# Expert gate and up products on one Trainium2 core: the token-lo blocks moved to the end of each bank, inside a branch of TensorE

## The chip, the cores and the metric

The kernel runs on one core of one Trainium2 chip. The metric is device time in microseconds (us) from the first to the last instruction; lower is better. All weights and inputs lie in DRAM as float32 when the kernel starts.

## The reference, cut to what matters

A two-layer decoder trunk over 256 tokens of width 1024. Layer 0 is a recurrent mixer with a dense SwiGLU, layer 1 a gated mixer with eight expert SwiGLUs of inner width 2816, of which every token uses the best two. The change concerns only the experts of layer 1:

```python
def swiglu(x, w_gu, w_down):
    gate, up = jnp.split(x @ w_gu, 2, axis=-1)
    return (jax.nn.silu(gate) * up) @ w_down

def moe_swiglu(x, w_router, w_gu, w_down):
    ...
    top_v, top_i = lax.top_k(logits, TOP_K)
    ...
    for e in range(N_EXPERTS):
        out = out + combine[:, e:e + 1] * swiglu(xt, w_gu[e], w_down[e]).astype(jnp.float32)
```

The 256 x 2 choices fall on all eight experts with the reference's own inputs (seed 0): 65, 55, 36, 28, 109, 103, 81 and 35 tokens, worked out from the reference's routing.

## The kernel before, in words

Every float32 product is made from rounded parts: a value is split into hi (rounded to the matmul's type) and lo (the rest), and a product is hi·hi + lo·hi + hi·lo, three matmuls into one accumulation in PSUM. For the experts the tokens of an expert are first gathered into 128 slots, which gives the blocks `xh` and `xl`, eight of each (128 rows of the 1024 each). These are the stationary side of the matmuls; the weights stream past them, 512 columns at a time.

The weights come by `Stream`. SP loads a piece of 2048 words a partition (1 MB) into one of the `raw` buffers. `part` (lines 119 to 128) splits 1024 words a partition of it: ScalarE writes the tile `hi` (line 127, `act.activation(h, v, AF.Copy)`), and then VectorE writes `lo` as the raw weights less `hi` (line 128). So a `lo` always follows its `hi`. The pool of `hi` tiles and the pool of `lo` tiles have four buffers each, by the 4 in line 831:

```python
    ws1 = Stream(ctx, "1", 1024, raws1, 4, "right")
```

An expert's `gate_up` (line 1162) goes over 2816 columns in five blocks of 512 and one of 256. For each it fills two PSUM banks called `gu`, first the gate, then the up columns. In this text a bank of 512 columns is a full bank, one of 256 a half bank. A full bank takes 1024 x 512 weights: four parts, each with two of the eight row blocks (k), and `lin_tm` (line 189) makes three matmuls for each row block, 24 in all. A half bank has two parts of four row blocks and also 24 matmuls, of 256 columns. `down` (line 1183) then takes 22 parts with six matmuls each, into the banks `py`.

`Feed.step` sets the order. It splits parts until those of this product are ready, issues the product, splits on until three parts (lead less one) of the next product are issued, calls `then()`, which issues what belongs to finished banks, and splits the fourth. `then()` after a gate bank issues the Silu on ScalarE (line 1176) and the transposes of the block before with their split (`hh` on ScalarE, line 224, `hl` on VectorE, line 225); after an up bank it issues the product of gate and up on VectorE (line 1178). In the first two steps of an expert it also issues the combination of the expert before (four matmuls and two VectorE additions a step, line 1256). ScalarE, VectorE and SP keep the order in which the program issues; TensorE's order is set by the scheduler.

After the experts a register is loaded from the largest count of tokens, and all engines jump over a second pass for experts with more than 128 tokens (lines 1298 to 1300).

Of the kernel before, what the change touches and what calls it, by code (L numbers as in the profile page):

```python
# [10 lines left out]
I32 = mybir.dt.int32  # L11
# [6 lines left out]
D = 1024  # L18
T = 256
KD = D // 128  # L20
# [12 lines left out]
def trunk(ctx: ExitStack, tc: tile.TileContext, a: dict, out: bass.AP, dbg=None, full=True):  # L33
# [31 lines left out]
    # ---------------------------------------------------------------- constants  # L65
# [12 lines left out]
    def preload(func):  # L78
        """The tables of an activation function, ahead of its first use."""
        act.activation(warm, ones[:, 0:1], func)  # L80
# [5 lines left out]
    # ---------------------------------------------------------------- weight stream  # L86
    class Stream:
        """Weights from DRAM in order, split into hi + lo parts of `size` words a partition."""
# [6 lines left out]
        def fetch(self, src):  # L95
            """Up to 2048 words a partition, [128, rows, columns]."""
            n1, n2 = src.shape[1], src.shape[2]
            raw = self.raws.pop(0)
            if raw not in self.once:
                self.raws.append(raw)  # L100
            v = raw()[:, :n1 * n2].rearrange("p (a b) -> p a b", a=n1)
            sp.dma_start(v, src)
            return v

        def split_parts(self, src, rows=None):
            """The parts of a piece of weights."""
            v = self.fetch(src)
            step = rows or self.size // v.shape[2]
            for k in range(0, v.shape[1], step):
                yield self.part(v[:, k:k + step, :])  # L110

        def fetch_cols(self, w, c0, n):
            """Columns c0..c0+n of w, in pieces of as many rows as fit."""
            if self.early:
                return self.early.pop(0)
            kk = min(KD, 2048 // n)
            return [self.fetch(w[k * 128:(k + kk) * 128, c0:c0 + n].rearrange("(k p) f -> p k f", p=128))
                    for k in range(0, KD, kk)]
# [12 lines left out]
        def blocks(self, w, c0, n):  # L131
            """Columns c0.. of w in blocks of 128, by rows k: [hi[k]], [lo[k]]."""
            vs = self.fetch_cols(w, c0, n)
            kk = vs[0].shape[1]
            width = min(n, max(128, self.size // kk))
            step = self.size // width
            for c in range(0, n, width):
                parts = [self.part(v[:, k:k + step, c:c + width]) for v in vs for k in range(0, kk, step)]
                for j in range(0, width, 128):
                    yield [[part[i][:, k, j:j + 128] for part in parts for k in range(step)] for i in range(2)]  # L140

        def cols(self, w, c0, n):
            """Columns c0..c0+n of w, by rows k: [hi[k]], [lo[k]]."""
            return self.split_cols(self.fetch_cols(w, c0, n))
# [6 lines left out]
        def rows(self, w, k0, nk):  # L151
            """Rows k0 * 128.. of w, by blocks of 128 rows."""
# [7 lines left out]
    class Feed:  # L160
        """Parts of weights, split `lead` parts ahead of their products."""
# [11 lines left out]
        def step(self, n, product, then):  # L173
            """The product with the next n parts; then() between the splits that come as these are used."""
# [7 lines left out]
    def lin_cm(o, w, x):  # L182
        """o[128 channels, T]: one block of 128 columns of w times x (hi and lo blocks)."""
        for k in range(KD):
            mm(o, w[0][k], x[0][k], k == 0, False)
            mm(o, w[1][k], x[0][k], False, False)
            mm(o, w[0][k], x[1][k], False, k == KD - 1)

    def lin_tm(o, w, x, t0, more=False):
        """o[128 tokens, columns]: x (hi and lo blocks) times columns of w."""  # L190
# [6 lines left out]
    def banks_cm(ws_, w, c0, n, x, piece=512, between=False):  # L197
        """Columns c0..c0+n of w times x, channels first: banks of two blocks; between: yields None between these."""
# [11 lines left out]
    def ahead(items):  # L210
        """The items, each once the one after it is under way."""
# [9 lines left out]
    def split(hi, lo, src, scale=None):  # L221
        """hi + lo = src * scale, exactly."""
# [7 lines left out]
    def rstd_of(pool_, ss, n, eps, name):  # L230
        """1 / sqrt(ss / n + eps)."""
# [10 lines left out]
    # ================================================================ layer 0: loads  # L242
# [43 lines left out]
    # ---------------------------------------------------------------- norms  # L286
    def rms(src, scr, both):
        """1 / rms of the rows of src [tokens, D]."""
# [9 lines left out]
    def turned(src, k, mm_bank):  # L298
        """Blocks k and k + 1 of src [tokens, D], channels first."""
# [6 lines left out]
    def normed(src, r, scaled, gain, n, mm_bank):  # L306
        """src * r * gain channels first, split; scaled: space for src * r."""
# [10 lines left out]
    class Norm:  # L318
        """RMS norm of xT as its blocks come: the blocks times the gain, split; the scale follows the products."""
# [7 lines left out]
        def squares(self, k, total):  # L327
            """total [128, 2, T]: the squares' sum over the blocks so far."""
# [10 lines left out]
        def scale(self, pl, ss=None):  # L339
            """1 / rms: a column per chunk of tokens, and across all partitions, twice."""  # L340
# [8 lines left out]
    # ---------------------------------------------------------------- memory attention  # L349
    def mem_kv(ws_, i, mh):  # L350
        """Yields between keys and values."""
# [9 lines left out]
    def mem_attn(i, qT, hi, lo, bank, sum_bank, tile, pr, together):  # L361
        """qT [128, 2, T] -> the two blocks hi, lo of the mixed activations; yields between pieces.
        tile(head), pr(head): space; together: all heads' scores before the first values."""
# [45 lines left out]
    # products that nothing reads, while x is loaded: they bring the tensor engine to its full clock  # L409
# [31 lines left out]
    # ================================================================ layer 0: time mixing  # L441
# [15 lines left out]
    def project(c0, whole):  # L457
        """Two blocks of columns; whole: in float32 as they are."""
# [64 lines left out]
    def per_head(o, r, n):  # L523
        """o[channels, n, 128 tokens] = r[tokens, 2 * n heads], each over its channels."""
# [66 lines left out]
    # inverses of the unit lower triangles: 16 rows by substitution, then merged in pairs, twice  # L591
    def fold(t):
        """24 pairs seen as two overlapping runs of 16: a leading dim of pairs to [2, 16]."""
# [32 lines left out]
    def block(out, l, r, i0, ni, c0, ncol, j0, nj):  # L626
        """out[i, c] = sum over j of l[i, j] * r[j, c], each given as (tile, offset, row's stride)."""
# [14 lines left out]
    # values, then values and keys tokens first, the values centered for the group norm  # L642
# [61 lines left out]
    # the states, chunk after chunk  # L704
# [35 lines left out]
    # the gate, times the group norm's weight, and times the bonus and the bias  # L740
# [27 lines left out]
    def group_norm(c0):  # L768
        """Group norm and gate of two chunks of tokens."""
# [21 lines left out]
    # memory keys and values of both layers, the attention of layer 0, and its mixed activations times w_out  # L791
# [18 lines left out]
    def mixed():  # L810
        """The mixed activations times w_out; yields between pieces of its columns."""
# [34 lines left out]
    # ---------------------------------------------------------------- dense SwiGLU  # L846
# [43 lines left out]
    # ================================================================ layer 1  # L890
# [87 lines left out]
    # ---------------------------------------------------------------- routing  # L978
# [11 lines left out]
    most_i = mr.tile([1, 1], I32, name="most_i")  # L990
    comb = mr.tile([128, 2, NE + 1], F32, name="comb")

    def slots(e0, base):
        """One-hot: the tokens of experts e0 and e0 + 1 in slots base.. ."""
# [11 lines left out]
    def routes(then):  # L1006
        """The two experts of each token, and its place among theirs."""
# [18 lines left out]
        dve.tensor_copy(most_i, most)  # L1026
        return dm, rest

    def gates():
        """The weights of the experts in the sum over them, and 1 / rms."""  # L1030
# [37 lines left out]
    def scaled(k, p):  # L1068
        """The block of columns times the gain; split, by what is returned."""
# [8 lines left out]
    def residual(k, p):  # L1078
        """Two blocks of the residual: with the mixed activations, in the routing's logits, and tokens first."""
# [36 lines left out]
    # ---------------------------------------------------------------- experts  # L1116
# [13 lines left out]
    def gather(e0, dm):  # L1130
        """The tokens of experts e0 and e0 + 1 in their slots: the experts' inputs, what makes a pair of blocks of
        these, and what makes the way back."""
# [29 lines left out]
    def gate_up(x, rs, hh, hl, step, at):  # L1162
        """silu(gate) * up, channels first, split. rs: 1 / rms of the slots' tokens."""
        for f in range(0, DFF, 512):
# [12 lines left out]
            step(KD * n // 1024, lambda w: lin_tm(ps[0], w, x, 0))  # L1177
            at(0, lambda: dve.scalar_tensor_tensor(sil, ps[1], rs, sil, op0=ALU.mult, op1=ALU.mult), True)
            at(1, turn)
            step(KD * n // 1024, lambda w: lin_tm(ps[1], w, x, 0))  # L1180

    def down(hh, hl, gw, step, at, last):
        """The expert's output, times the gates, split; last(o, c, y) for a half of its columns and a chunk of tokens."""
# [45 lines left out]
    def final_gain():  # L1229
        """In the space of a load."""  # L1230
# [7 lines left out]
    def finish(c, o):  # L1238
        """What the final norm can have before all squares are summed."""
# [18 lines left out]
    def experts(base, feed):  # L1258
        ahead_ = []

        def at(i, f, front=False):
            """f at the end of the step i from now."""
# [15 lines left out]
        for e in range(NE):  # L1278
# [5 lines left out]
            gate_up((xh, xl), gw[:, 1:2], hh, hl, step, at)  # L1284
# [17 lines left out]
    # ---------------------------------------------------------------- final norm  # L1302
# [34 lines left out]
```

## Time and profile before

| | |
|---|---|
| Median of 2 runs | 1339.28 us (1334.67 and 1343.89) |
| Profiled execution, its span | 1343.8 us (the run of 1343.89) |
| TensorE busy | 1312.2 us, 98% |
| VectorE busy | 1048.5 us, 78% |
| ScalarE busy | 894.8 us, 67% |
| DRAM to SBUF | 351 MB, 261 GB/s on average |
| The experts' stage | about 542 to 1330 us |

PE is TensorE's matmuls and PEld its loads of the stationary side, which overlap the matmuls; DVE is VectorE, ACT ScalarE. A matmul's end is modelled: matmuls are pipelined, and the time from start to start says what one takes in a row of them. [...]

### The profile page before, as it was taken

The page shows a single profiled execution, that of the slowest core. Times are in us where ns is not written, and L with a number is a line of the kernel's source. Part 1 is how long each engine was busy: PE and PEld are TensorE (multiplying, and loading weights), DVE is VectorE, ACT ScalarE, POOL GpSimd, SP SyncE. Part 2 cuts the span into 40 slices and gives each one's busy share as a digit, 9 for nine tenths or more (in the row PEclk, how much of TensorE's full clock was granted, in tenths as well). Part 3 has the DMA queues.
Part 4 walks back from the last instruction along what each step waited for, and adds up shares of the span by engine and source line. Part 5 has one row for each costly group of instructions (what it writes and reads, how often), then busy time and mean ns, then how long its engine had stood idle before and what let it go on. Part 6 is the DMA issues. An engine that isn't in the chain of part 4 may idle for free. (4 is left out here: it accounts for less than half of the span.)

```text
span 1343.8 us, 20395 instructions
## 1 busy us (share of the span) xinstructions
PE 1312.2 (98%) x7968; PEld 1130.8 (84%) x7968; DVE 1048.5 (78%) x1257; ACT 894.8 (67%) x1160; POOL 19.8 (1%) x40
## 2 busy tenths in 40 slices
PE   8998999999999998999999999999999999999996
PEld 7987778999999888788888888888888888888884
DVE  4789525666654775899997998997999987999996
ACT  6614416744443765887787887777777777777775
POOL 2000000000000100000000000000000000000000
PEclk8998959999999999999999999999999999999998
DMA  5512103755555844899999999999999999999970
GB/s 183 168 52 95 33 1 133 275 188 189 191 188 188 302 157 148 314 333 372 336 360 333 336 359 369 339 358 322 327 367 377 350 350 321 347 354 378 352 278 34
DMA packets 170648, 351.32 MB, mean 261 GB/s; under 512 B 5796, under 2 KB 46848, under 8 KB 170544
## 3 DMA queue, kind: packets, MB, share of 16 engines
q1 hardware_dynamic: 169216, 346.05, 72.7%
q0 software_dynamic: 1280, 3.88, 0.9%
q8 instruction: 64, 1.05, 0.3%
q14 instruction: 40, 0.33, 0.1%
q10 hardware_dynamic: 48, 0.01, 0.0%
HBM read 348.87 MB, written 1.05 MB: 260 GB/s over the span
## 5 line engine op out<-in xcount | busy, mean ns | idle before, releaser
L128 DVE TENSOR_TENSOR lo<-raw,hi 128x1024 fp32r<-128x1024 f32 (+1 forms) x636 | 737.0, 1201 | 140.0 <-ACT hi L127 138.6
L127 ACT ACTIVATE hi<-raw 128x1024 fp32r<-128x1024 f32 (+1 forms) x636 | 644.5, 1045 | 181.6 <-PE gu L58 58.4
L58 PE MATMUL gu<-hi,xh 128*128 128x512 f32 (+1 forms) x768 | 289.4, 377 | 0.0
L58 PE MATMUL gu<-hi,xl 128*128 128x512 f32 (+1 forms) x768 | 289.1, 376 | 0.0
L58 PE MATMUL gu<-lo,xh 128*128 128x512 f32 (+1 forms) x768 | 287.9, 377 | 0.0
L58 PEld LDWEIGHTS gu<-hi,xh 128*128 128x128 f32 x768 | 144.5, 188 | 27.9 <-ACT hi L127 0.2
L58 PEld LDWEIGHTS gu<-hi,xl 128*128 128x128 f32 x768 | 144.3, 188 | 28.0
L58 PEld LDWEIGHTS gu<-lo,xh 128*128 128x128 f32 x768 | 144.3, 188 | 27.4 <-DVE lo L128 0.2
L58 PE MATMUL lin<-nh,lo 128*128 128x256 f32 x528 | 151.6, 287 | 5.4 <-DVE lo L128 5.4
L58 PE MATMUL lin<-nh,hi 128*128 128x256 f32 x528 | 151.9, 288 | 0.5 <-DVE rT L446 0.2
L58 PE MATMUL lin<-nl,hi 128*128 128x256 f32 x528 | 151.0, 286 | 0.0
L58 PE MATMUL py<-hi,hh 128*128 128x512 f32 x352 | 140.4, 399 | 0.0
L58 PE MATMUL py<-hi,hl 128*128 128x512 f32 x352 | 139.5, 396 | 0.0
L58 PE MATMUL py<-lo,hh 128*128 128x512 f32 x352 | 111.1, 397 | 0.0
L58 PEld LDWEIGHTS lin<-nh,lo 128*128 128x128 f32 x528 | 101.3, 192 | 7.1 <-DVE lo L128 5.8
L58 PEld LDWEIGHTS lin<-nh,hi 128*128 128x128 f32 x528 | 101.2, 192 | 2.8 <-issue 0.7
L58 PEld LDWEIGHTS lin<-nl,hi 128*128 128x128 f32 x528 | 101.5, 192 | 1.0 <-issue 0.6
L58 PEld LDWEIGHTS py<-lo,hh 128*128 128x128 f32 x352 | 66.1, 188 | 16.3 <-DVE lo L128 0.5
L58 PEld LDWEIGHTS py<-hi,hh 128*128 128x128 f32 x352 | 66.3, 188 | 14.8
L58 PEld LDWEIGHTS py<-hi,hl 128*128 128x128 f32 x352 | 66.3, 188 | 14.8
L1176 ACT ACTIVATE sil<-gu,gw 128x512 f32<-128x512 f32 (+1 forms) x48 | 31.5, 655 | 42.7 <-PE gu L58 41.3
L225 DVE TENSOR_TENSOR hl<-mm,hh 128x512 fp32r<-128x512 f32 (+1 forms) x48 | 31.0, 646 | 25.8 <-ACT hh L224 25.8
(408 smaller groups left out, 1587.2 us busy)
## 6 DMA issues: line engine op xcount, KB each, us to landing
raw<-in_moe_w_gu SPq DMA_DIRECT2D x174, 1024.0 KB, 6.7
raw<-in_moe_w_down SPq DMA_DIRECT2D x87, 1024.0 KB, 6.9
raw<-in_ffn_w_gu SPq DMA_DIRECT2D x22, 1024.0 KB, 6.7
raw<-in_ffn_w_down SPq DMA_DIRECT2D x11, 1024.0 KB, 5.0
raw<-in_w_out SPq DMA_DIRECT2D x7, 1024.0 KB, 9.9
raw<-in_gmlp_w_in SPq DMA_DIRECT2D x7, 1024.0 KB, 5.3
raw<-in_rwkv_w_in SPq DMA_DIRECT2D x5, 1024.0 KB, 5.1
rawa<-in_rwkv_w_in SPq DMA_DIRECT2D x3, 1024.0 KB, 6.8
```

The costliest lines, as they stand in the source:

```text
L58: pe.matmul(o, l, r, start=start, stop=stop, skip_group_check=loose)
L127: act.activation(h, v, AF.Copy)
L128: dve.tensor_tensor(l, v, h.bitcast(F32), op=ALU.subtract)
L225: dve.tensor_tensor(lo, src, hi.bitcast(F32), op=ALU.subtract)
L1176: at(0, lambda: act.activation(sil, ps[0], AF.Silu, scale=rs), f > 0)
```

## The change

`gate_up` calls a new `lin_some` in place of `lin_tm`. For each of the eight row blocks it makes the two products of `xh` (with the weights' hi and with their lo); the eight products of `xl` with the weights' hi come after all of these, under a condition that the expert's count of tokens is above zero. The condition's body has TensorE's instructions alone. The counts, which the routing has in PSUM, are copied to integers on VectorE, and each expert loads its own into a register of TensorE. There are 96 such conditions in one pass over the experts, and eight register loads. The other engines get a plain jump at each of them. The diff also takes out comments and docstrings, which make no instruction.

```diff
@@ gate and up of an expert
-    def gate_up(x, rs, hh, hl, step, at):
+    def lin_some(o, w, x, n):
+        for k in range(KD):
+            mm(o, x[0][k], w[0][k], k == 0, False, True)
+            mm(o, x[0][k], w[1][k], False, k == KD - 1, True)
+        with tc.If(n > 0):
+            for k in range(KD):
+                mm(o, x[1][k], w[0][k], False, k == KD - 1, True)
+
+    def gate_up(x, rs, hh, hl, step, at, count):
...
-            step(KD * n // 1024, lambda w: lin_tm(ps[0], w, x, 0))
+            step(KD * n // 1024, lambda w: lin_some(ps[0], w, x, count))
...
-            step(KD * n // 1024, lambda w: lin_tm(ps[1], w, x, 0))
+            step(KD * n // 1024, lambda w: lin_some(ps[1], w, x, count))
@@ routing
+    count_i = mr.tile([1, NE], I32, name="count_i")
...
         dve.tensor_copy(most_i, most)
+        dve.tensor_copy(count_i, pl[0:1, 2 * NE:3 * NE])
@@ experts
-            gate_up((xh, xl), gw[:, 1:2], hh, hl, step, at)
+            count = nc.values_load(count_i[0:1, e:e + 1], engines=[mybir.EngineType.PE], min_val=0, max_val=T)
+            gate_up((xh, xl), gw[:, 1:2], hh, hl, step, at, count)
```

How the change moves instructions is seen at the second gate bank of the first expert. TensorE before, the last two of its four parts (`hi` and `lo` with neighbouring numbers are one part) and the start of the up bank behind it:

```order
L58 MATMUL gu_5727<-hi_5718,xh_5567 128x512
L58 MATMUL gu_5727<-hi_5718,xl_5568 128x512
L58 MATMUL gu_5727<-lo_5719,xh_5567 128x512
L58 MATMUL gu_5727<-hi_5723,xh_5567 128x512
L58 MATMUL gu_5727<-hi_5723,xl_5568 128x512
L1172 MATMUL mm_5771<-ident_83,sil_5624 128x128
L58 MATMUL gu_5727<-lo_5724,xh_5567 128x512
L58 MATMUL gu_5727<-hi_5723,xh_5567 128x512
L58 MATMUL gu_5727<-hi_5723,xl_5568 128x512
L58 MATMUL gu_5727<-lo_5724,xh_5567 128x512
```

Each part is used in six matmuls on end, and a part's `hi` is read for the last time at its fifth.

TensorE now, the same bank from its last part on, to the first matmuls of the up bank:

```order
L58 MATMUL gu_5741<-hi_5737,xh_5569 128x512
L1183 MATMUL mm_5786<-ident_83,sil_5636 128x128 x4
L58 MATMUL gu_5741<-lo_5738,xh_5569 128x512
L58 MATMUL gu_5741<-hi_5737,xh_5569 128x512
L58 MATMUL gu_5741<-lo_5738,xh_5569 128x512
L1169 COMPARE_AND_BRANCH
L58 MATMUL gu_5741<-hi_5722,xl_5570 128x512 x2
L58 MATMUL gu_5741<-hi_5726,xl_5570 128x512 x2
L58 MATMUL gu_5741<-hi_5732,xl_5570 128x512 x2
L58 MATMUL gu_5741<-hi_5737,xl_5570 128x512 x2
L1169 UNCONDITIONAL_BRANCH x2
L58 MATMUL gu_5742<-hi_5771,xh_5569 128x512
```

All four `hi` tiles of the bank are read once more behind the branch, the first of them (`hi_5722`) at the 17th and 18th matmul of 24. One of the two jumps ends the body, the other stands in the path of an expert without tokens.

ScalarE now, the four parts of this bank, and those of the up bank behind the jump:

```order
L127 ACTIVATE hi_5722<-raw11_5720 128x1024
L127 ACTIVATE hi_5726<-raw11_5720 128x1024
L127 ACTIVATE hi_5732<-raw20_5730 128x1024
L127 ACTIVATE hi_5737<-raw20_5730 128x1024
L1169 UNCONDITIONAL_BRANCH
L127 ACTIVATE hi_5771<-raw21_5769 128x1024
L127 ACTIVATE hi_5775<-raw21_5769 128x1024
L127 ACTIVATE hi_5781<-raw22_5779 128x1024
L1187 ACTIVATE sil_5743<-gu_5741,gw_5572 128x512
L224 ACTIVATE hh_5622<-mm_5786 128x512
L127 ACTIVATE hi_5793<-raw22_5779 128x1024
```

ScalarE's own order is as before but for the jump; with four buffers, `hi_5771` goes where `hi_5722` was.

## Rows read from the trace of the kernel before

**Rows 1.** Windows: stretch, busy us of PE, PEld, DVE, ACT, POOL, clock, DMA share, GB/s

```profile
600.00:700.00 100.00, 100.00 (x483) 82.72 (x482) 92.38 (x88) 78.67 (x84) 0.00 (x0) 1.00 0.99 359
```

**Rows 2.** Waits, 600 to 1300 us: who waited for whom, total us, times, longest

```profile
ACT hi L127 <- PE gu L58: 53.9, 130, 1.5
DVE lo L128 <- ACT hi L127: 47.8, 116, 3.2
...
PEld py L58 <- DVE lo L128: 0.5, 2, 0.3
```

**Rows 3.** Timeline of TensorE, two matmuls of one bank, start and length in us

```profile
645.75 0.40 PE L58 MATMUL gu<-hi,xl 128*128 128x512 f32 x1
...
648.77 0.39 PE L58 MATMUL gu<-lo,xh 128*128 128x512 f32 x1
```

**Rows 4.** Timeline of ScalarE in gate and up, with the idle time ahead

```profile
646.19 1.06 ACT L127 ACTIVATE hi<-raw 128x1024 fp32r<-128x1024 f32 x1 [0.33 <-PE gu L58]
...
655.70 0.69 ACT L1176 ACTIVATE sil<-gu,gw 128x512 f32<-128x512 f32 x1 [0.57 <-PE gu L58]
...
656.77 2.98 ACT L127 ACTIVATE hi<-raw 128x1024 fp32r<-128x1024 f32 x3
...
667.27 0.69 ACT L1176 ACTIVATE sil<-gu,gw 128x512 f32<-128x512 f32 x1 [0.57 <-PE gu L58]
```

**Rows 5.** Timeline of VectorE in gate and up

```profile
650.47 1.28 DVE L1256 TENSOR_TENSOR x<-mm,x 128x512 f32<-128x512 f32 x2
651.67 4.73 DVE L128 TENSOR_TENSOR lo<-raw,hi 128x1024 fp32r<-128x1024 f32 x4
...
657.86 4.63 DVE L128 TENSOR_TENSOR lo<-raw,hi 128x1024 fp32r<-128x1024 f32 x4 [0.26 <-ACT hi L127]
662.41 0.75 DVE L1178 SCALAR_TENSOR_TENSOR sil<-gu,gw,sil 128x512 f32<-128x512 f32 x1
663.07 3.51 DVE L128 TENSOR_TENSOR lo<-raw,hi 128x1024 fp32r<-128x1024 f32 x3
```

**Rows 6.** Timeline near the end: a split on the heels of ScalarE's copy

```profile
1317.18 1.07 ACT L127 ACTIVATE hi<-raw 128x1024 fp32r<-128x1024 f32 x1 [0.34 <-PE py L58]
...
1318.28 1.23 DVE L128 TENSOR_TENSOR lo<-raw,hi 128x1024 fp32r<-128x1024 f32 x1 [0.18 <-ACT hi L127]
```

**Rows 7.** Timeline near the end: TensorE starts again after a wait for VectorE

```profile
1330.19 0.74 DVE L228 SCALAR_TENSOR_TENSOR ys<-py,gw,ys 128x512 fp32r<-128x512 f32 x1
...
1330.99 0.72 PE L58 MATMUL gu<-ys,dT 128*128 128x512 f32 x2 [0.62 <-DVE ys L228]
```

**Rows 8.** Timeline of TensorE in a half bank

```profile
700.22 0.28 PE L58 MATMUL gu<-hi,xh 128*128 128x256 f32 x1
700.33 0.28 PE L58 MATMUL gu<-hi,xl 128*128 128x256 f32 x1
```

**Rows 9.** Timeline of VectorE across the register load and the jump behind the experts

```profile
1334.04 0.08 DVE L1246 DVE_READ_ACCUMULATOR sq<-x 128x1 f32 x1
1336.92 0.16 DVE L1304 TENSOR_TENSOR ss<-ssf 128x2 f32<-128x2 f32 x1 [2.81 <-DVEq L1299]
```

**Rows 10.** Timeline of TensorE's weight loads in the first gather

```profile
540.16 0.54 PEld L58 LDWEIGHTS gu<-dm,ngh 128*128 128x128 f32 x4 [0.42 <-ACT xh L1142]
```

**Rows 11.** Timeline of TensorE: two idle stretches in layer 0 and what ended them

```profile
28.13 1.31 PE L58 MATMUL mm<-lora,early 64*128 64x256 f32 x4 [1.57 <-ACT sg L504]
...
137.50 1.71 PE L58 MATMUL acc<-T,G 32*32 32x32 f32 x96 [1.25 <-DVE T L640]
```

**Rows 12.** Windows around these stretches, columns as in rows 1

```profile
28.40:28.80 0.40, 0.40 (x3) 0.34 (x3) 0.40 (x2) 0.40 (x3) 0.00 (x0) 1.00 0.00 0
...
29.20:29.60 0.40, 0.40 (x2) 0.23 (x2) 0.40 (x2) 0.40 (x2) 0.00 (x0) 0.50 0.00 0
...
32.40:32.80 0.40, 0.40 (x3) 0.35 (x3) 0.00 (x0) 0.40 (x1) 0.00 (x0) 1.00 0.00 0
...
138.50:139.00 0.50, 0.50 (x44) 0.50 (x38) 0.50 (x2) 0.45 (x2) 0.20 (x1) 1.00 0.00 0
```

## The prediction, made before the changed kernel was run

> **What bounds the kernel now.** I read the windows first. [...] Busy alone does not say who leads, so the waits come next: in 700 us of this stage ScalarE waits 53.9 us for TensorE to be done with a `hi` buffer, VectorE waits 47.8 us for ScalarE's `hi`, and TensorE's longest wait for a `lo` is one of 0.3 us, 0.5 us in all [rows 2]. So TensorE bounds the stage, and the split runs ahead of it, held back only by the four buffers. The timelines show the rhythm: a matmul of 512 columns every (648.77 - 645.75) / 13 = 0.232 us [rows 3]. A gate and an up bank together take 667.27 - 655.70 = 11.57 us from Silu to Silu, 5.79 us a bank [rows 4]; 48 matmuls are 11.14 of this, and the transposes the other 0.43.
>
> **The change part by part.** The number of matmuls is the same, and each row block is loaded as often as before. No expert of the reference's inputs is without tokens, so nothing is skipped. What changes is when a `hi` buffer comes free. Before, the first part of a bank is read for the last time at the 5th of 24 matmuls, the second at the 11th, and ScalarE can write the next bank's parts while this bank still runs. Now all four are read again at the end, the first until the 18th matmul, the fourth until the 24th. ScalarE cannot begin the next bank's first `hi` before the 18th, and VectorE's `lo` follows `hi`. TensorE needs that `lo` as the second matmul of the next bank. So the split no longer runs beside the bank before; most of it lies between the banks.
>
> The time from one bank's 18th matmul to the next bank's, step by step:
> - Release: the last matmul that reads a `hi` starts at 645.75, and ScalarE's next copy starts at 646.19: 0.44 us [rows 3, 4].
> - First `hi`: from its start at 1317.18 to the `lo` that waits for it at 1318.28, 1.10 us [rows 6].
> - VectorE's four `lo`: four on end take 4.63 us, and one alone 1.23, so a step is 1.13 [rows 5, 6]. Between the third and the fourth stands one other operation, the product of gate and up (from 662.41 to the next `lo` at 663.07, 0.66 [rows 5]) or the `hl` split, which I put at the same. From the first start to the fourth end: 3 x 1.13 + 0.66 + 1.23 = 5.28 us. ScalarE is faster: copies follow at (2.98 - 1.06) / 2 = 0.96 us, and with Silu and `hh` ahead of the fourth (655.70 to 656.77, 1.07) [rows 4] that one ends 5.0 us after the first starts, 0.1 us ahead of its `lo`.
> - TensorE starts again: 0.06 us after VectorE's end at 1330.93, and the pair there takes 0.72 us where 0.40 + 0.23 would do: 0.06 + 0.09 = 0.15 us [rows 7].
> - From the matmul with the fourth `lo` to the 18th: two more of the last row block, then two of `xl`, 4 x 0.232 = 0.93 us.
>
> Sum: 0.44 + 1.10 + 5.28 + 0.15 + 0.93 = 7.90 us, against 5.79, so +2.11 us. The transposes fit in TensorE's idle time: it gets to the fourth `lo` 0.4 us early with them in. An expert has nine such steps (ten full banks): 19.0 us.
>
> The half banks close the gate and up. From the last up bank's 18th matmul to their end, before: 6 x 0.232 + 48 x 0.116 [rows 8] + 0.43 = 7.4 us. Now the gate half's second `lo` is there after 0.44 + 1.10 + 1.13 + 1.23 = 3.90 us; with 0.15 to start, seven matmuls of the part, eight of `xl` and then the up half with the transposes (0.81, 0.93, 2.78, 0.43) the end is at 9.0: +1.6 us. In `down` nothing is moved: six matmuls a part are 1.39 us against VectorE's 1.13, and the split gets ahead again before the next expert.
>
> The combination of the expert before puts two additions (1.20 us, 650.47 to 651.67 [rows 5]) into VectorE's row in each of two steps, +1.7 us in all where the split is late; its eight matmuls, 1.86 us before, now fall into idle time. I count the two as equal.
>
> Together 8 x (19.0 + 1.6) = 165 us.
>
> The branches. Each bank has a compare ahead of `xl` and a jump behind. The order shows a wait of TensorE only in the path of an empty expert. When the compare comes, TensorE still has three matmuls of the last part, 0.70 us, and the jump has the eight of `xl`, 1.86 us; these hide both, and I take nothing. Without that cover, the nearest row bounds it from above: VectorE's 2.81 us behind the experts, which hold a register load, a compare and a jump over a whole second pass [rows 9]. The lower end is nothing. The jumps on ScalarE and VectorE come where both wait anyway.
>
> [...]
>
> The eight register loads stand in TensorE's queue in the first gather, around the products with `comb`. The lower end is nothing, since TensorE waits for ScalarE there anyway (0.42 us before 540.16 [rows 10]); the upper is 8 x 2.81 = 22 us [rows 9]. That row holds a load and more, so I take 1 us each, less what the wait hides: 7 us. SP has nothing new but jumps; loads are issued as `lo` frees the raw buffers, later than before, and the DMA engines get slack.
>
> Sum: 165 + 7 = 172 us on the profiled execution's 1343.9, 1516 us. That execution is 4.6 us above the median of the two runs shown, so on the median 1339.3 + 172 = 1511 us, 13% slower.
>
> **The rivals.**
>
> *The branches are not hidden.* A compare and a jump could hold TensorE's sequencer so long that the queue runs dry. For it: the 2.81 us on VectorE. Against it: that jump goes over a pass of hundreds of instructions, these over two. If each bank paid the whole row, less the 0.70 us of cover, 96 x 2.1 = 203 us come on top: about 1714; at half a microsecond beyond the cover, 1559.
>
> [...]
>
> *The clock falls.* Now TensorE idles about 0.9 us ahead of each bank's first `lo`, and some 2 us a bank in all. In layer 0 it idled 1.57 us until 28.13, and from 29.20 the clock was 0.50 (1.2 GHz), until it was full again at 32.40; an idle stretch of 1.25 us that ended at 137.50 left it at 1.00 [rows 11, 12]. Gaps of 0.9 us are shorter than both, which speaks against. If it fell in each bank for some 3 us, half of these, 1.6 us, would be lost, of which the idle time takes back up to 0.9: 0.7 to 1.6 us in 80 full banks, some 90 us: about 1600.
>
> *Not slower: the split still keeps ahead.* For it: TensorE hardly ever waits now, and ScalarE idles a fifth of the time. The step where it decides is the next bank's first `lo`: if this were ready when the 24th matmul has started and gone (6 x 0.232 = 1.4 us after the 18th), TensorE would go on as before. It would need a fifth buffer or an earlier release; the chain above has it at 0.44 + 1.10 + 1.23 = 2.8 us. Then only the loads remain: 1339 + 7 = 1346 us, within 2%.
>
> *The condition skips work.* With an empty expert eight of 24 matmuls go. But the four `lo` are still late: its step would lose only the two `xl` matmuls of 7.90, so even that expert would be slower than before. The counts have none; I give it nothing.
>
> **How the numbers follow.** The forecast has 0.72, the branches 0.10, the clock 0.12, not slower 0.03, and 0.03 is left for what I don't see (half of it faster by some rearrangement of TensorE's order). The forecast's own ends: a step shorter by 0.5 us (the restart hidden, the operation between the `lo` moved aside) is 36 us less, without the loads 43, so 1470 in round numbers; with 22 us of loads and 0.3 us more a step, 1550. The range goes on to 1610 to hold the clock's case and the smaller branch cases. A measurement can tell about 2% from no change (27 us): slower by more than that in all but the not-slower case and the remainder: slower 0.96, same 0.03, faster 0.01.
>
> **What would show it.** Right: TensorE's waits for `lo`, hardly there before, become the largest of the stage, about 2 us a full bank and over 100 us in all; ScalarE's copies come in runs of three and four right behind a bank's 18th matmul, where before one came every 1.4 us; Silu to Silu takes about 15.8 us; `down` takes as long as before; DMA share and VectorE's share fall. Wrong: idle time at the branch line with `lo` long ready (branches), a clock under 1.00 in the stage (clock), or Silu to Silu still near 11.6 us (not slower).

## The result, and the profile after the change

| | before | after |
|---|---|---|
| Median of 2 runs | 1339.28 us (1334.67 to 1343.89) | 1511.68 us (1509.03 to 1514.33) |
| Ratio, 95% interval | | 1.1246 (1.1170 to 1.1322) |
| Profiled execution, its span | 1343.8 us | 1512.5 us |

The changed kernel is slower by 12.5%; the forecast was 1511 us. First the same stretch of windows as in [rows 1], in the profile after:

```profile
600.00:700.00 100.00, 90.99 (x394) 66.95 (x392) 76.20 (x74) 62.84 (x69) 0.00 (x0) 1.00 0.87 302
```

TensorE makes 394 matmuls where it made 483, at the same granted clock of 1.00, the full one. In the whole execution it makes 7968, as before, so nothing was skipped. All the other engines and the DMA are less busy too, so none of them has become the bound: the stage has turned into a chain of waits. These are the waits of the same 700 us as in [rows 2]:

```profile
ACT hi L127 <- PE gu L58: 212.2, 69, 5.2
DVE lo L128 <- ACT hi L127: 181.9, 123, 2.6
PEld gu L58 <- DVE lo L128: 140.3, 215, 1.3
```

The first two were there before, at 53.9 and 47.8 us. The third is new: TensorE, which waited 0.5 us for `lo`, now waits 140 us with its weight loads. Fewer and longer waits of ScalarE (69 of up to 5.2 us, where it had 130 of up to 1.5) say that the `hi` buffers now come free in bunches.

One bank after the other shows it. In the timeline of the three engines the columns are start and length in us, engine, line and operation, and in brackets the idle time ahead and what ended it:

```profile
704.84 1.98 PE L58 MATMUL gu<-hi,xl 128*128 128x512 f32 x8
705.50 3.91 ACT L127 ACTIVATE hi<-raw 128x1024 fp32r<-128x1024 f32 x4 [2.86 <-PE gu L58]
706.59 3.50 DVE L128 TENSOR_TENSOR lo<-raw,hi 128x1024 fp32r<-128x1024 f32 x3 [2.60 <-ACT hi L127]
707.87 0.50 PE L58 MATMUL gu<-lo,xh 128*128 128x512 f32 x1 [0.77 <-DVE lo L128]
...
710.00 0.75 DVE L1189 SCALAR_TENSOR_TENSOR sil<-gu,gw,sil 128x512 f32<-128x512 f32 x1
...
710.66 1.22 DVE L128 TENSOR_TENSOR lo<-raw,hi 128x1024 fp32r<-128x1024 f32 x1
...
711.94 0.50 PE L58 MATMUL gu<-lo,xh 128*128 128x512 f32 x1 [0.16 <-DVE lo L128]
712.27 0.40 PE L58 MATMUL gu<-hi,xh 128*128 128x512 f32 x1
712.51 0.40 PE L58 MATMUL gu<-lo,xh 128*128 128x512 f32 x1
712.74 2.00 PE L58 MATMUL gu<-hi,xl 128*128 128x512 f32 x8
713.40 2.96 ACT L127 ACTIVATE hi<-raw 128x1024 fp32r<-128x1024 f32 x3 [4.00 <-PE gu L58]
```

The `xl` matmuls begin at 704.84. The second of them (704.84 + 0.23 = 705.07) is the last reader of the first `hi` tile, and only then, at 705.50, may ScalarE write the next bank's four parts, in one run. VectorE follows each, TensorE waits for every `lo` (the matmul behind such a wait shows 0.50 us: 707.87, 709.00, 710.14 and 711.94), and the eight `xl` follow the last pair without a gap: no idle time stands at the branch. Before, ScalarE's copies were spread over the bank and VectorE's four `lo` ran ahead of TensorE [rows 4, 5].

ScalarE's rows from the second expert's first bank on, and two Silu of gate banks:

```profile
664.40 2.96 ACT L127 ACTIVATE hi<-raw 128x1024 fp32r<-128x1024 f32 x3 [2.77 <-PE gu L58]
...
672.84 3.91 ACT L127 ACTIVATE hi<-raw 128x1024 fp32r<-128x1024 f32 x4 [3.96 <-PE gu L58]
...
681.94 2.96 ACT L127 ACTIVATE hi<-raw 128x1024 fp32r<-128x1024 f32 x3 [5.18 <-PE gu L58]
...
716.27 0.67 ACT L1187 ACTIVATE sil<-gu,gw 128x512 f32<-128x512 f32 x1
...
721.23 3.91 ACT L127 ACTIVATE hi<-raw 128x1024 fp32r<-128x1024 f32 x4 [2.86 <-PE gu L58]
...
732.00 0.67 ACT L1187 ACTIVATE sil<-gu,gw 128x512 f32<-128x512 f32 x1
```

Silu to Silu is 15.73 us, where [rows 4] had 11.57. The runs of copies follow each other after 7.90 us (705.50 to 713.40, with the product of gate and up in VectorE's row) and 7.83 us (713.40 to 721.23, with the `hl` split there): 7.87 us a bank on average, against 5.79.

### The profile page after: what moved, and what is told of

It reads as the page before. It is cut to its first block, busy times and chain, and to the rows that moved or that the text cites. A ratio compares the mean times of both kernels' runs of the same rounds, so it can differ in the third digit from the quotient of the medians.

```text
span 1512.5 us, 20557 instructions
## 1 busy us (share of the span) xinstructions
PE 1387.8 (92%) x7968; PEld 1111.4 (73%) x7968; DVE 1047.4 (69%) x1258; ACT 878.3 (58%) x1160; POOL 19.7 (1%) x40
## 5 line engine op out<-in xcount | busy, mean ns | idle before, releaser
L127 ACT ACTIVATE hi<-raw 128x1024 fp32r<-128x1024 f32 (+1 forms) x636 | 633.1, 1038 | 407.4 <-PE gu L58 287.8
L58 PE MATMUL gu<-lo,xh 128*128 128x512 f32 (+1 forms) x768 | 316.6, 418 | 91.0 <-DVE lo L128 91.0
L58 PE MATMUL gu<-hi,xl 128*128 128x512 f32 (+1 forms) x768 | 179.0, 376 | 0.0
L58 PEld LDWEIGHTS gu<-hi,xl 128*128 128x128 f32 x768 | 137.6, 189 | 27.4
L58 PE MATMUL acc<-hh,hi 128*128 128x256 f32 x132 | 36.8, 279 | 0.0
L58 PE MATMUL acc<-hh,lo 128*128 128x256 f32 x132 | 36.8, 279 | 0.0
```

The source lines that it names most:

```text
L58: pe.matmul(o, l, r, start=start, stop=stop, skip_group_check=loose)
```

## The experiments

Besides the median, each kernel is read by the time of one expert: the start of the first gate matmul of the second and of the eighth expert in its timeline of TensorE, a sixth of what lies between. This leaves out layer 0, after which the first expert starts anywhere from 531.58 to 553.88 us in these traces (last section), and the first expert itself.

| kernel | time, us | second expert | eighth expert | one expert, us |
|---|---|---|---|---|
| before | 1339.28 | 636.95 | 1232.11 | 99.19 |
| after | 1511.68 | 659.45 | 1380.22 | 120.13 |
| same order, no condition | 1513.35 | 657.52 | 1377.01 | 119.92 |
| conditions, old order | 1346.72 | 636.42 | 1231.42 | 99.17 |
| after, 5 `hi` buffers | 1440.98 | 659.13 | 1316.05 | 109.49 |
| after, 6 `hi` buffers | 1361.98 | 630.35 | 1244.24 | 102.31 |
| after, 8 `hi` buffers | 1361.77 | 637.34 | 1246.15 | 101.47 |
| after, operations behind the fourth split | 1452.18 | 652.64 | 1325.33 | 112.11 |
| after, both of the last two | 1347.66 | 640.43 | 1234.14 | 98.95 |

The rows of the kernel before and then of the changed one, on which the first two lines rest, with the first expert's start ahead of them:

```profile
542.20 0.40 PE L58 MATMUL gu<-hi,xh 128*128 128x512 f32 x1
...
636.95 0.40 PE L58 MATMUL gu<-hi,xh 128*128 128x512 f32 x1
...
1232.11 0.40 PE L58 MATMUL gu<-hi,xh 128*128 128x512 f32 x1
```

```profile
542.13 0.40 PE L58 MATMUL gu<-hi,xh 128*128 128x512 f32 x1
...
659.45 0.39 PE L58 MATMUL gu<-hi,xh 128*128 128x512 f32 x1
...
1380.22 0.39 PE L58 MATMUL gu<-hi,xh 128*128 128x512 f32 x1
```

The first four experiments below ran on one chip, beside 13 runs of the kernel before with a median of 1344.68 us (1333.73 to 1354.10); the last four on another, beside 13 with 1349.37 us (1340.31 to 1355.93).

**The order without the condition.** The `xl` matmuls stay last in the bank; the condition and the register loads go.

```diff
-        with tc.If(n > 0):
-            for k in range(KD):
-                mm(o, x[1][k], w[0][k], False, k == KD - 1, True)
+        for k in range(KD):
+            mm(o, x[1][k], w[0][k], False, k == KD - 1, True)
...
-            count = nc.values_load(count_i[0:1, e:e + 1], engines=[mybir.EngineType.PE], min_val=0, max_val=T)
+            count = None
```

Expected:

> The order of the changed kernel, with the xl products last in each bank, but without conditions, jumps and register loads. Buffer theory (the late release of the hi tiles costs the time): 1505 to 1517 us, Silu to Silu 15.7 us a pair of banks, as in the changed kernel. Branch rival (compares and jumps hold TensorE): back to 1339 to 1350 us, 11.6 us a pair.

Measured: 1513.35 us (one run), an expert 119.92 us. The largest wait of TensorE in 600 to 1300 us is that of the changed kernel:

```profile
PEld gu L58 <- DVE lo L128: 139.9, 214, 1.3
```

The order alone costs the loss. With the conditions an expert of twelve banks takes 0.21 us more, 0.02 us for each of them.

**The conditions without the order.** All 96 conditions and eight loads stay; only the last row block's `xl` matmul is inside, the other seven are back at their old places.

```diff
         for k in range(KD):
             mm(o, x[0][k], w[0][k], k == 0, False, True)
+            if k < KD - 1:
+                mm(o, x[1][k], w[0][k], False, False, True)
             mm(o, x[0][k], w[1][k], False, k == KD - 1, True)
         with tc.If(n > 0):
-            for k in range(KD):
-                mm(o, x[1][k], w[0][k], False, k == KD - 1, True)
+            mm(o, x[1][KD - 1], w[0][KD - 1], False, True, True)
```

Expected:

> 96 conditions and 8 register loads as in the changed kernel, but each holds only the xl product of the last row block; the other seven stand where they were. Buffer theory: hi tiles come free as before but for the fourth (24th matmul, not 23rd), so 1339 to 1350 us; what it is above the kernel before is the price of conditions, jumps and loads, which the prediction put at 7 us, all of it the loads. Branch rival: about 1512 us.

Measured: 1346.72 us (1342.42 to 1359.63, 10 runs), ratio to before 1.0036 (0.9994 to 1.0078). The first expert starts at 541.70 us (542.20 before), and TensorE is busy throughout; its windows, in the columns of [rows 1]:

```profile
600.00:700.00 100.00, 100.00 (x481) 82.66 (x480) 92.16 (x89) 78.65 (x85) 0.00 (x0) 1.00 0.98 359
```

This is the row of the kernel before but for a matmul or two, and an expert takes 99.17 us against 99.19. Twelve conditions an expert cost nothing that can be seen here, where matmuls stand queued on both sides of them.

**Eight `hi` buffers.** If the late release is the cause, a second set of four buffers takes it away. Two of the ten raw buffers go for the room.

```diff
-    ws1 = Stream(ctx, "1", 1024, raws1, 4, "right")
+    ws1 = Stream(ctx, "1", 1024, raws1, 4, "right", 8)
...
-    ws.raws += [raw_buffer(ctx, f"raw2{i}", 2048, "right") for i in range(4)]
+    ws.raws += [raw_buffer(ctx, f"raw2{i}", 2048, "right") for i in range(2)]
```

(The new last argument sets the buffers of `hi` alone.) Expected:

> The changed kernel with eight hi buffers in place of four (the space comes from two of ten raw buffers). Buffer theory: the next bank's hi tiles have places of their own, the split runs beside the bank before, 1340 to 1360 us. Branch rival: stays at 1505 to 1520 us.

Measured: 1361.77 us (one run), 2 us above the range given: 150 of the 172 us are back, by the expert 18.7 of 20.9, with the order and the conditions as in the changed kernel. What is left shows in the waits (600 to 1300 us) and in ScalarE's timeline:

```profile
ACT sil L1187 <- PE gu L58: 118.7, 41, 4.4
...
PEld gu L58 <- ACT hi L127: 16.8, 27, 0.8
```

```profile
773.20 0.69 ACT L1187 ACTIVATE sil<-gu,gw 128x512 f32<-128x512 f32 x1 [3.26 <-PE gu L58]
...
774.26 7.72 ACT L127 ACTIVATE hi<-raw 128x1024 fp32r<-128x1024 f32 x8
785.25 0.69 ACT L1187 ACTIVATE sil<-gu,gw 128x512 f32<-128x512 f32 x1 [3.27 <-PE gu L58]
```

ScalarE, now ahead, stands at the Silu for 3.3 us until the gate bank is finished, and the fourth `hi` of the next bank stands behind it in the program's order. Silu to Silu is 12.05 us, 0.48 over [rows 4]; five such pairs in each of eight experts are 19 us. TensorE's waits for `hi` come about once a pair (27 in 700 us, in which seven experts make 35 pairs). The last experiment tries this reading.

**The kernel before with two raw buffers fewer**, the control for the room:

```diff
-    ws.raws += [raw_buffer(ctx, f"raw2{i}", 2048, "right") for i in range(4)]
+    ws.raws += [raw_buffer(ctx, f"raw2{i}", 2048, "right") for i in range(2)]
```

Expected:

> Control: the kernel before with the same two raw buffers taken away and nothing else. Both theories: 1335 to 1355 us, since TensorE bounds the experts and the loads have eight raw buffers left.

Measured: 1341.58 us (one run), inside the range of the kernel before; an expert takes 99.21 us (632.37 to 1227.61 for six). The room that the buffers took is not what the other runs show.

**Five `hi` buffers**, the edit above with 5 in place of 8. Expected:

> The changed kernel with five hi buffers in place of four (and two of the ten raw buffers fewer, which room this takes and which by itself cost nothing). Theory (the late release of the hi buffers sets the step): the next bank's first hi needs no release any more, its second waits for the release at the 18th matmul, so only three lo and the one other operation follow the release: 0.44 + 1.10 + (2 x 1.13 + 0.66 + 1.23 = 4.15) + 0.15 + 0.93 = 6.77 us a bank in place of 7.90, 1.13 less; over 72 steps 81 us less than the changed kernel: about 1425 us (1400 to 1440). Silu to Silu 13.5 us. ScalarE's wait for TensorE falls from 267 us to about 190. Rival (what costs is the order of the matmuls in itself, or the lo being needed as the second matmul, whatever the buffers): 1500 to 1515 us.

Measured: 1440.98 us (one run), 1 us above the range given. The step itself is as worked out: ScalarE's copies behind a release start at these times,

```profile
692.92 2.01 ACT L127 ACTIVATE hi<-raw 128x1024 fp32r<-128x1024 f32 x2 [2.85 <-PE gu L58]
...
706.50 2.01 ACT L127 ACTIVATE hi<-raw 128x1024 fp32r<-128x1024 f32 x2 [2.88 <-PE gu L58]
```

13.58 us for two banks (one more run starts between them, at 699.72), 6.79 a bank against 6.77 expected. The experts only started later, at 553.88 us where before had 542.20; without these 11.7 us it would be 1429. They come from layer 0, whose granted clock was lower in this execution (last section).

**Six `hi` buffers.** Expected:

> The changed kernel with six hi buffers (two raw buffers fewer). Theory: two lo and the other operation follow the release, 0.44 + 1.10 + (1.13 + 0.66 + 1.23 = 3.02) + 0.15 + 0.93 = 5.64 us, under the 5.79 us that the 24 matmuls and transposes take, so TensorE is the bound again: 1340 to 1375 us, as with eight buffers (1361.8). Silu to Silu 11.6 to 12.0 us. Rival (each further buffer brings the same until eight): about 1425 less another 30 to 40, 1390 us.

Measured: 1361.98 us (one run), an expert 102.31 us. That this is the time of eight buffers is chance: the experts began at 531.58 us here and at 538.51 there, and 0.84 us more for each expert take up this lead. The gain does not come buffer by buffer: four to five brings 10.6 us an expert, five to six 7.2, six to eight 0.8. It ends about where the chain, by the sum above 5.64 us, gets shorter than the 5.79 us of a bank's matmuls and transposes.

**The operations of finished banks behind the fourth split**, with four `hi` buffers:

```diff
-            self.upto(self.lead - 1)
-            then()
             self.upto(self.lead)
+            then()
```

Expected:

> The changed kernel with four hi buffers, but the operations that belong to finished banks (Silu and hh on ScalarE, the product of gate and up and hl on VectorE) issued after the fourth split of the next bank and not between the third and the fourth. Theory (VectorE's row of four lo with the one operation in it lies wholly between the banks): 0.66 us less a step, 7.24 us, so 72 x 0.66 = 48 us less than the changed kernel: about 1464 us (1450 to 1480), Silu to Silu 14.5 us. Rival (the step hangs on ScalarE's copies, or on TensorE's release alone): 1500 to 1515 us.

Measured: 1452.18 us (one run), 12 us less than worked out. ScalarE's runs start at

```profile
693.24 3.90 ACT L127 ACTIVATE hi<-raw 128x1024 fp32r<-128x1024 f32 x4 [2.30 <-PE gu L58]
700.47 3.90 ACT L127 ACTIVATE hi<-raw 128x1024 fp32r<-128x1024 f32 x4 [3.32 <-PE gu L58]
```

7.23 us apart, against 7.24 expected: one VectorE operation of 0.66 us in the row of `lo` was worth exactly its time. An expert takes 8.0 us less; nine steps of 0.66 are 5.9. I had left out that the combination's additions go behind the fourth split too. In the changed kernel they lengthen the second expert's first two steps by 1.80 us (next section); here these two are as short as the others, 7.23 and 7.25 us:

```profile
657.03 3.91 ACT L127 ACTIVATE hi<-raw 128x1024 fp32r<-128x1024 f32 x4 [2.44 <-PE gu L58]
...
664.26 3.90 ACT L127 ACTIVATE hi<-raw 128x1024 fp32r<-128x1024 f32 x4 [2.76 <-PE gu L58]
671.51 3.90 ACT L127 ACTIVATE hi<-raw 128x1024 fp32r<-128x1024 f32 x4 [3.34 <-PE gu L58]
```

5.9 and 1.80 are 7.7 of the 8.0 us.

**Eight `hi` buffers and the operations behind the fourth split**, both edits. Expected:

> The changed kernel with eight hi buffers and with the operations of finished banks issued after the fourth split. With eight buffers alone 1361.8 us were left, 17 to 20 more than before. Theory for that rest (ScalarE keeps its order, waits for a bank's end at the Silu, and only then writes the fourth hi of the next bank, for which TensorE then waits): the fourth hi is written ahead of the Silu, TensorE does not wait, and the time is that of the kernel before, 1335 to 1350 us, with TensorE's waits for hi (25 us with eight buffers alone) near nothing. Rival (the conditions, or something else that the order brings, costs the rest): 1358 to 1365 us.

Measured: 1347.66 us (1336.61 to 1359.14, 10 runs), ratio to before 0.9961 (0.9912 to 1.0009). Its Silu and copies:

```profile
760.66 0.69 ACT L1186 ACTIVATE sil<-gu,gw 128x512 f32<-128x512 f32 x1 [3.48 <-PE gu L58]
...
772.20 0.69 ACT L1186 ACTIVATE sil<-gu,gw 128x512 f32<-128x512 f32 x1 [2.56 <-PE gu L58]
```

ScalarE still stands at the Silu, but now nothing that TensorE needs next is behind it: Silu to Silu is 11.54 us again and an expert 98.95. From 600 to 1300 us TensorE's gate and up no longer wait for a `hi`. In the first expert they still do (7.1 us in all), and that one takes 98.78 us where it took 94.75 before. So with the new order, all conditions and all loads in place, the kernel is as fast as before once the buffers and the order of ScalarE let the split run ahead. It is no faster: TensorE has the same matmuls to make and is the bound again, and no kernel tried here beat the one before.

## Why the prediction was right, step by step

**What bounds the kernel.** Confirmed. TensorE led before [rows 1, 2], and what it lost is what the kernel lost.

**The step of a full bank.** The five terms, forecast and read from the timeline above:

| term | forecast | measured | from |
|---|---|---|---|
| release | 0.44 | 0.43 | 705.07 to 705.50 |
| first `hi` | 1.10 | 1.09 | 705.50 to 706.59 |
| four `lo` and the one operation | 5.28 | 5.29 | 706.59 to 710.66 + 1.22 = 711.88 |
| TensorE starts again | 0.15 | 0.16 | 711.88 to 711.94, and 0.33 where 0.23 would do |
| last four matmuls | 0.93 | 0.93 | 711.94 to 712.74 + 0.23, less 0.10 |
| sum | 7.90 | 7.90 | with the `hl` split in place of the product 7.83 |

Each term came from a row of the kernel before in which the same hand-over happened once by itself, and each held to within 0.01 us.

**The half banks.** Two rows each, of the kernel before and of the changed one, bound this part: the matmul that is the last full bank's 18th (or, after, the first of the `xl` row, of which the 18th is the second), and the first of `down`:

```profile
694.62 0.40 PE L58 MATMUL gu<-lo,xh 128*128 128x512 f32 x1
...
702.33 0.39 PE L58 MATMUL py<-hi,hh 128*128 128x512 f32 x1
```

```profile
736.31 1.98 PE L58 MATMUL gu<-hi,xl 128*128 128x512 f32 x8
...
746.01 0.39 PE L58 MATMUL py<-hi,hh 128*128 128x512 f32 x1
```

After: 746.01 - 736.54 = 9.47 us, of which two `py` matmuls that the scheduler put in between take 0.46, so 9.0 as forecast. Before: 7.71 us, not 7.4; I had left out the 18th matmul's own 0.23 us. The difference is 1.3, not 1.6. `down` takes as long as before, as forecast: from its first matmul to the third expert's first 738.51 - 702.33 = 36.2 us before, 781.94 - 746.01 = 35.9 after, with those two matmuls of 0.46 us already made.

**The combination.** Forecast: 1.7 us in VectorE's row, given back by its matmuls falling into idle time. The two steps that hold it run from 664.40 to 672.84 and to 681.94: 8.44 and 9.10, together 1.80 us over two plain ones.

**The branches.** Forecast nothing, and next to nothing was found, three times over: taken away (119.92 us an expert against 120.13), put in alone (99.17 against 99.19), and with the order repaired (98.95). The bound of 2.81 us from the jump behind the experts [rows 9] was far too high for these short jumps. The trace of the changed kernel has them on the queue of TensorE's weight loads (PEldq). The columns are the count, then the shortest, middle and longest in ns, then the first and last start in us; the second line has 711 to 713 us alone, the bank shown in the result:

```profile
L1169 PEldq COMPARE_BRANCH  x192: 65/130/307, 542.5 to 1464.5; - x192
...
L1169 PEldq COMPARE_BRANCH  x2: 65/117/169, 711.9 to 712.1; - x2
```

Each condition has two jumps. Both of this bank have ended by 712.3 us, while the matmuls ahead of `xl` still run; the first `xl` starts at 712.74. The cover that I named, matmuls queued on both sides, is there in all three kernels; a condition without it was not tried.

The two of this bank take 0.065 and 0.169 us, 0.23 together. Twelve such pairs would be 2.8 us an expert (an estimate from these two times), if TensorE had to stand still for them; the 99.17 us against 99.19 say that it did not.

**The register loads.** This is the term that was mis-sized: 7 us forecast, 1.0 us found at most. The trace of the changed kernel has all eight, 0.30 us each and the first 0.49, and the kernel before had one on the same queue, behind the experts, a nearer row than [rows 9]:

```profile
L1295 PEldq TENSOR_LOAD <-count_i x8: 297/304/491, 534.2 to 539.4; - x8
```

```profile
L1298 PEldq TENSOR_LOAD <-most_i x1: 487/487/487, 1331.1 to 1331.1; - x1
```

They run beside the matmuls of the first gather. From the gather's first matmul to the first gate matmul TensorE takes 542.13 - 534.00 = 8.13 us with them, and 541.22 - 534.08 = 7.14 us in the kernel without conditions and loads. Part of this 1.0 us is the clock, which in the second kernel was back at 1.00 some half a microsecond earlier (0.76 against 0.52 from 537 to 538 us). That the wait for ScalarE in the gather [rows 10] covers the rest of the loads is the likely reason; no run took that wait away. The first expert's start by itself (542.13 us with loads, 542.20 before) does not tell, since it has all of layer 0 in it.

**What I missed.** The first expert takes 659.45 - 542.13 = 117.32 us against 636.95 - 542.20 = 94.75: 22.6 more, where the others take 20.9 more. From one bank's `xl` to the next, its first two steps last 9.17 and 8.96 us (545.87 to 555.04, and to 564.00), without any combination:

```profile
545.87 1.99 PE L58 MATMUL gu<-hi,xl 128*128 128x512 f32 x8
...
551.29 0.69 ACT L1187 ACTIVATE sil<-gu,gw 128x512 f32<-128x512 f32 x1 [1.32 <-DVE gw L1155]
551.87 1.05 ACT L127 ACTIVATE hi<-raw 128x1024 fp32r<-128x1024 f32 x1
552.97 0.51 PE L58 MATMUL gu<-hi,xh 128*128 128x512 f32 x1 [0.84 <-ACT hi L127]
...
555.04 3.57 PE L58 MATMUL gu<-hi,xl 128*128 128x512 f32 x8
...
558.45 0.40 PE L58 MATMUL gu<-hi,xh 128*128 128x512 f32 x1
```

```profile
555.00:558.00 3.00, 3.00 (x8) 2.33 (x7) 0.73 (x1) 1.16 (x2) 0.00 (x0) 0.50 0.83 254
```

In the first step a Silu waits for the expert's weights `gw`, the fourth `hi` stands behind it, and TensorE waits for that. In the second the granted clock was 0.50 for about 3 us: eight `xl` matmuls took 3.57 us in place of 1.98. From start to start they are (558.45 - 555.04) / 8 = 0.426 us each, 1.20 columns a nanosecond, which is the trace's number for the 1.2 GHz of the prediction; at 1.00 the 0.232 us of [rows 3] are 2.2 columns a nanosecond. Just before, TensorE had waited 0.84 us for this `hi` and 0.76 us for its `lo`. The kernel without conditions shows the same fall at the same place (0.51 from 554.6 to 558.0 us), the kernel before does not.

**The sum.** Forecast 165 us for the experts and 7 for the loads; the spans differ by 1512.5 - 1343.8 = 168.7, all of it from the first expert's start on. An expert takes 20.9 us more, not 20.6, and the first one another 1.6. That the median came within 1 us of the forecast is partly luck: 4 us too few in the experts, 6 to 7 too many for the loads, and two medians of two runs each.

**The rivals.** "The branches are not hidden" fell by the two kernels that part order and conditions. "The clock falls" came true once, for about 3 us in the first expert; from 600 to 1300 us the granted clock was 1.00, and gaps of 0.77 us ahead of each bank's first `lo` left it there. Priced at some 90 us, it cost less than 2. "Not slower" named its own deciding point, a fifth buffer or an earlier release; the runs with more buffers show that the point was right, and that it takes six buffers to get near it. "The condition skips work" had no empty expert and was not tried.

## What to carry to other kernels

When matmuls are regrouped, look up for each buffer who reads it last in the new order, and count from that reader to the first one who needs the next content; if this chain is longer than the work that is left in between, every group pays the difference, however idle the other engines look. Here the same instructions in another order cost 21 us an expert with four buffers and nothing with eight, once the engine that fills them did not have to finish something else first. So a branch that is meant to skip work must first be placed where not skipping costs nothing.

## What the runs showed that was not expected

- The busy share hides part of a loss. TensorE shows 91% busy in the window above, so 9 us of 100 idle, while an expert lost 20.9 of 120.1 us. A matmul behind a wait is shown as 0.50 us and the next starts 0.33 us after it (711.94 to 712.27), where 0.23 is the rhythm. The count of matmuls (394 against 483, 18% less), the busy time of PEld (66.95 against 82.72 us, 19% less) and its waits, 140 us in 700, tell it better.
- With buffers to spare, program order on ScalarE costs by itself: 0.48 us a pair of banks for one copy behind a Silu that waits, gone when the copy went first.
- Layer 0, up to its dense SwiGLU the same work in all of these kernels, runs at different granted clocks in different executions. These two windows are from the kernel before and from the one with five `hi` buffers:

```profile
100.00:200.00 100.00, 93.11 (x974) 76.18 (x972) 59.95 (x98) 35.58 (x83) 1.46 (x2) 0.79 0.13 43
```

```profile
100.00:200.00 100.00, 93.43 (x929) 76.08 (x927) 61.00 (x101) 34.66 (x81) 1.46 (x2) 0.73 0.13 43
```

The granted clock was 0.73 there against 0.79, and 0.92 in the next 100 us (0.97 before); in the kernel with six `hi` buffers it was 0.88 and 1.00. The experts began at 553.88 us with five buffers and at 531.58 with six. The 22 us between these two starts are a little more than the spread of the kernel before over 13 runs (20 and 16 us). What sets the clock there was not looked into. A comparison of a later stage is best made from that stage's own start.
